# Small matrix products brought to the array's full height and width

## The chip, the cores and the metric

The kernel runs on one core of a Trainium2 chip. The time is the device time of one execution in microseconds: 2515.39 as the median of three runs (2513.62 to 2515.6). A profile was taken of one execution.

## The reference

Two transformer blocks over 256 tokens, model width 2048, float32. The first block puts 16 meta tokens ahead (272 positions). Its layer A is a differential attention: 8 heads, two score maps each of head size 128, `w = softmax(s0) - lambda * softmax(s1)`, times values of size 256, a norm, a gate, an output projection. Its layer B is an attention with sinks: 32 query heads of size 64, 4 key heads, four chunks of 64 queries; a chunk sees the 16 meta tokens and up to three chunks of keys, so 80, 144, 208 and 208 keys:

```python
sr = jnp.einsum('bnqkgd,bnskd->bnkgqs', qr, kb).astype(jnp.float32) * scale
pr = sink_softmax(sr, sink[None, None, :, :, None, None])
orr = jnp.einsum('bnkgqs,bnskd->bnqkgd', pr.astype(v.dtype), vb).reshape(B, S, D_MODEL)
```

The second block mixes a stick-breaking attention, a forgetting attention (4 heads of 128 each) and an RWKV-7 recurrence of 16 heads of size 64, whose decay and rate come from two low-rank products over 64 features (`tanh(wd) @ w_up`, `ad @ a_up`). Then come branch and output projections and an MLP of width 8192.

## The kernel before

**Main products.** The weights come as units of 2048 x 128 (one DMA of 1 MB each). ACT rounds a quarter of a unit to a short format (`wh`), DVE subtracts it (`wl`), and PE sums high x high, high x low and low x high products for every block of 128 rows (`unit_mm`, line 689). A product with both operands in the short format (F32R) is one instruction; an unsplit float32 product is two, called passes below. Main products have 128 rows, 128 columns of weights and 272 or 256 moving columns. Up to eight quarters of split weights can lie ready (WBUFS).

**Side work.** The attentions and the recurrence are generators that are moved on between main products; each `yield` is a place where another may go on. The order is made when the program is written out: each engine runs its calls in the order they are made, and `tick` (line 486) keeps an estimate of each engine's clock that decides when a step or a split of weights may follow. `limit` (line 598) finishes all but some pieces of a kind at once, whatever the clock says.

**Shapes on PE.** A form such as 64*128 in the trace means 64 rows (the summed dimension, on the partitions) and 128 columns of weights. The places that the change touches:

- `g_av` (949) and `g_attn_a` (965), layer A. The scores of the first 16 queries are a product with 16 columns of weights and 16 moving columns. The parts of the values and of the weights of the first 16 keys (high, low, high) are stacked to 48 rows, transposed as blocks of 48 columns, for the 16 queries as a block of 16 rows, and multiplied as a 48-row F32R product at the head of each half of the weighted sum.
- `e_kk` (1149), `g_bk` (1164), `g_q` (1207), `g_attn_b` (1223), layer B. For the chunks 0 and 1 the scores are unsplit 64-row products. For the chunks 2 and 3 the query's high and low parts are stacked to 128 rows and meet the key's high parts, which stand twice; then the query's high parts alone, 64 rows, meet the key's low parts. Both take 256 moving columns, more than the 208 that are used. In the weighted sum the last 16 keys of chunk 1 are a product of 16 rows; all its products have 64 columns, two heads beside each other.
- `e_lo` (1390), `g_r1` (1514). The two up projections are each a 128-row product (weights' high and low parts against the features' high parts, which stand twice) and a 64-row one (weights' high parts against the features' low parts).

In time the layers follow each other: layer A's heads run beside its own projections, layer B's beside its query and gate units (16 pairs of heads, `g_attn_b` once a pair), the recurrence's first stage beside its eight `rr`, `rk`, `rv` groups.

Of the kernel before, what the change touches and what calls it, by code (L numbers as in the profile page):

```python
# [20 lines left out]
S = 256  # L21
# [10 lines left out]
# the sets of function tables that hold a function  # L32
# [155 lines left out]
def unit_rows(inp, kind, i):  # L188
    """the unit's weights as [16 * 128 rows, 128 columns]"""
# [16 lines left out]
def const_arrays():  # L206
# [32 lines left out]
    # stage 1 of the recurrence: causal masks of the chunk products, chunk starts  # L239
# [7 lines left out]
    # stick-breaking and forgetting attention  # L247
# [8 lines left out]
def prepare(inp):  # L256
# [37 lines left out]
    # a head's rows of the forget sums' high and low parts  # L294
# [17 lines left out]
class _Eng:  # L312
    """an engine's builders, with a running estimate of when each call ends"""
# [26 lines left out]
class Prog:  # L340
# [40 lines left out]
    def rel(self, n=1):  # L381
        """the last use of n side banks is out"""
        self.live -= n
# [34 lines left out]
    def mm(self, out, lhsT, rhs, start=True, stop=True, beside=False):  # L418
        """beside: in the array's other columns, while the product before it runs"""
# [43 lines left out]
    def split_to(self, n):  # L463
        """the weights' first n pieces are split"""
        while self.done < n:
            if self.high == self.done:
                self.split_high()
            self.split_low()

    def fill(self):  # L470
        """split the weights: what is needed soon, and further while the engines are idle"""
# [12 lines left out]
    # Each engine runs its calls in the order they are made.  The estimate of every  # L484
    # engine's clock decides when a piece of side work may follow the main products.
    def tick(self, eng, attr, args, kw):
        out = kw.get("out", args[0] if args else None)
        if eng == "PE":
# [4 lines left out]
            else:  # L493
                n = _free(out)
                cost = 25.0 if self.beside else 110.0 * n / 256 if kw["rhs"].dtype == F32R else max(1.69 * n, 105.0 if _free(kw["lhsT"]) <= 64 else 213.0)
# [30 lines left out]
    def wait(self, ns):  # L526
        """the piece's next part follows a transfer of about this long"""
# [5 lines left out]
    # how many pieces of a kind may be under way together  # L533
# [33 lines left out]
    def room(self, n):  # L567
        """side work goes on until n side banks are free"""
# [3 lines left out]
    def step_gens(self):  # L572
        """move the side work on as far as its inputs are ready by now"""
# [24 lines left out]
    def limit(self, names, n):  # L598
        """let at most n pieces of such side work stay unfinished"""
# [9 lines left out]
    def run(self):  # L609
        nsub = NSUB  # L610
        self.raw, self.wsplit, self.free = {}, {}, []
        # when the first units' pieces have come
# [3 lines left out]
        # units taken together where their moving operand comes late  # L616
# [8 lines left out]
        for group in groups:  # L625
            jobs = []
            for v in group:
# [11 lines left out]
                if "join" in spec:  # L639
                    # the unit goes on with the sums of the one before  # L640
# [48 lines left out]
    def unit_mm(self, kb, b, job, w):  # L689
        """a block's products: high x high, high x low, low x high"""  # L690
# [3 lines left out]
        if spec.get("flip"):  # L694
# [5 lines left out]
            if v >= len(self.order) - 2:  # L700
                # the last units end one half of the tokens before they take up the other
# [20 lines left out]
    def evacuate(self, force=False):  # L722
        """the finished units' products leave PSUM, once their token scales are there"""
# [6 lines left out]
    def start(self):  # L730
# [25 lines left out]
        # a layer's operand comes later to this room  # L756
# [40 lines left out]
    def g_scalars(self):  # L797
        """-lambda and the scaled copies of subln's gain and of the sinks"""
# [33 lines left out]
    def newton(self, y, x):  # L832
        """one step of y -> x ** -0.5"""
# [15 lines left out]
    def tok_rsqrt(self, x):  # L849
        """x ** -0.5 for a small tile with tokens on the partitions"""  # L850
# [15 lines left out]
    def tok_spread(self, ps, dg, blocks):  # L866
        """ps[:, block] = the block's scales, on every partition"""
# [3 lines left out]
    def rsqrt_ps(self, out, ps, scale, eps_col):  # L871
        """out = (ps * scale + eps) ** -0.5"""
# [33 lines left out]
    def x_ak(self, i):  # L906
        d = self.x_A(i)
        if i == 0:
            # a quarter of the operand is there before the products, the next ones go on beside them
# [4 lines left out]
    def rope_evac(self, out, ps, t0, n, quads):  # L914
        """out = rope(ps * R) for the token columns t0..t0+n"""
# [21 lines left out]
    def e_av(self, i, ps):  # L937
# [4 lines left out]
        if f == 0:  # L942
            self.avt[h] = self.t("avt", [128, 2, 2, 128], bufs=2), self.t("av16", [48, 2, 128], F32R)
# [5 lines left out]
    def g_av(self, h, f, vT):  # L949
        # the parts of the first 16 tokens, to meet high, high and low  # L950
        v3 = self.t("av3", [128, 48], F32R)
# [5 lines left out]
        self.tr(pv[0:48, 256:384], v3.bitcast(F32), 128)  # L957
# [4 lines left out]
        self.act(self.avt[h][1][:, f, :], pv[0:48, 256:384], AF.Copy)  # L962
        self.rel()

    def g_attn_a(self, h):
# [4 lines left out]
        for j in range(2):  # L970
# [4 lines left out]
            self.mm(s[0:16, 416:432], q[:, 0:16], k[:, 0:16])  # L975
# [31 lines left out]
        w3 = self.t("aw3", [128, 3, 48], F32R)  # L1007
# [11 lines left out]
        self.tr(p2[0:48, 0:16], w3[0:16, 2], 16)  # L1019
        self.tr(p2[0:48, 16:144], w3[:, 0], 128)  # L1020
        self.tr(p2[0:48, 144:272], w3[:, 1], 128)
        yield
        wt = self.t("awt", [128, 384], bufs=1)
        w16 = self.t("aw16", [48, L], F32R, bufs=1)
        self.act(wt, p1[:, 0:384], AF.Copy)
        self.act(w16, p2[0:48, 0:L], AF.Copy)
# [44 lines left out]
    def g_gate(self, i, G, h, f):  # L1071
# [4 lines left out]
        # 2 * G * sigmoid(G)  # L1076
# [57 lines left out]
    # key columns are kept in the order chunk 0, meta, chunk 1, 2, 3: the keys of every  # L1134
    # chunk's queries are then one run of columns
# [3 lines left out]
    def rope_b(self, ps, t0):  # L1139
        """the two terms of rope(ps * R) for the tokens from t0 on"""  # L1140
# [8 lines left out]
    def e_kk(self, i, ps):  # L1149
        if i == 0:  # L1150
            self.finish(self.tabs)
            self.bk = self.t("bk", [64, 4, L], bufs=1)
            # high parts, twice in the rows, and low parts
            self.bkh = self.t("bkh", [128, 4, L], F32R, bufs=1)
            self.bkl = self.t("bkl", [64, 4, L], F32R, bufs=1)
        t, tmp = self.rope_b(ps, 0)
        self.mul(tmp, tmp, self.SR)
        for hh in range(2):
            hs = slice(64 * hh, 64 * hh + 64)
            for a, b, o in self.SEGS:  # L1160
                self.add(self.bk[:, 2 * i + hh, a:b], t[hs, o:o + b - a], tmp[hs, o:o + b - a])
        self.spawn(self.g_bk(slice(2 * i, 2 * i + 2)))

    def g_bk(self, ks):
        yield
        for j in range(2):
            self.act(self.bkh[64 * j:64 * j + 64, ks], self.bk[:, ks], AF.Copy)
        self.sub(self.bkl[:, ks], self.bk[:, ks], self.bkh[0:64, ks].bitcast(F32))
# [38 lines left out]
    def g_q(self, i, t, tmp):  # L1207
        yield
        self.mul(tmp, tmp, self.SR[:, NM:])
        q = self.t("bq", [64, 4, 2, 64], bufs=3)  # L1210
# [4 lines left out]
        # the later chunks' high and low parts, stacked  # L1215
        qs = self.t("bqs", [128, 2, 128], F32R, bufs=3)
        q2 = q[:, 2:4].rearrange("p c e x -> p c (e x)")
# [3 lines left out]
        self.bgen[i] = self.spawn(self.g_attn_b(i, q, qs))  # L1221

    def g_attn_b(self, i, q, qs):
        """two heads: rows are (head, query of the chunk)"""
# [4 lines left out]
        s = [s0[:, 0:80], s0[:, 80:224], s0[:, 224:432], s1[:, 48:256]]  # L1229
        for c, (a, b) in enumerate(self.KEYS[0:2]):  # L1230
            self.mm(s[c], q[:, c].rearrange("p e x -> p (e x)"), self.bk[:, kv, a:b])
# [972 lines left out]
```

## Time and profile before

| | |
|---|---|
| median of three runs | 2515.39 us |
| profiled execution, span | 2513.7 us |
| PE busy | 2475.5 us (98%), 19842 matmuls |
| DVE busy | 1706.6 us (68%) |
| ACT busy | 1413.9 us (56%) |
| POOL busy | 186.0 us (7%) |
| DMA | 452.66 MB, 180 GB/s |

The busy time of a matmul runs from its start to a modelled end, and matmuls overlap: a main product of 256 columns is shown with some 280 ns and followed by the next after some 118 ns. What one costs is therefore read from the starts. All instructions carry the line of one helper (L325), so they are told apart by their tiles: `pg` is the sum of a main product, `ps` of a side product.

### The profile page before, as it was taken

Reading aid. Unit: us, or ns where it says so; the run is one execution under the profiler, and the core shown is the slowest. Engines: PE = TensorE matmul, PEld = TensorE weight load, DVE = VectorE, ACT = ScalarE, POOL = GpSimd, SP = SyncE. Lnnn points to the kernel's source line nnn. Section 1 sums busy time; section 2 is a strip of 40 time slices with the busy share of each in tenths; the row PEclk is TensorE's granted clock in tenths of the full one; section 3 lists DMA queues with packets and bytes.
Section 4 is the critical chain, followed back from the end, with each engine's and each line's share of the span. In section 5 each row is a group of like instructions: output and inputs, shape, how many; then the busy total and the mean of one; then the engine's idle time right before and its main releaser. Section 6 shows DMA issues by size and latency. Waiting matters only on the chain.

```text
span 2513.7 us, 50471 instructions
## 1 busy us (share of the span) xinstructions
PE 2475.5 (98%) x19842; PEld 2358.2 (94%) x19842; DVE 1706.6 (68%) x3347; ACT 1413.9 (56%) x2888; POOL 186.0 (7%) x230
## 2 busy tenths in 40 slices
PE   8999999999999999999999999999899999999998
PEld 7999999999999999999999999999899899899886
DVE  8666676667777667777795568766765666666665
ACT  5555555557666667666555436445655455455444
POOL 5110001010000120000000100111200000000002
PEclk9999999999999999999999999999999999999999
DMA  6344444543333454667645764755455555555553
GB/s 232 138 165 151 152 153 154 181 173 135 135 135 135 168 196 174 202 203 226 216 179 174 235 195 171 279 213 186 151 185 184 186 188 192 190 185 185 188 191 125
DMA packets 123647, 452.66 MB, mean 180 GB/s; under 512 B 54704, under 2 KB 65968, under 8 KB 73872
## 3 DMA queue, kind: packets, MB, share of 16 engines
q1 hardware_dynamic: 123216, 449.24, 50.8%
q8 instruction: 156, 2.56, 0.4%
q14 instruction: 83, 0.68, 0.1%
q0 software_dynamic: 192, 0.18, 0.0%
HBM read 431.55 MB, written 17.83 MB: 179 GB/s over the span
## 4 chain that ended last, share of the span: by engine, by line
PE 96%; DVE 2%; ACT 0%; DMA 0%; issue 0%; POOL 0%; DVEq 0%; SPq 0%; ACTq 0%; POOLq 0%
PE pg L325 79%; PE ps L325 18%; DVE wl L325 0%; DMA h<-in_h_dram 0%; DVE xml L325 0%; DVE h L325 0%; DVE acc L325 0%; ACT wh L325 0%; DVE pr L325 0%; DVE xl L325 0%; ACT uj L325 0%; ACT xh L325 0%; ACT xmh L325 0%; DVE nt L325 0%; POOL gl L325 0%
## 5 line engine op out<-in xcount | busy, mean ns | idle before, releaser
L325 DVE TENSOR_TENSOR wl<-wr,wh 128x512 fp32r<-128x512 f32 x1556 | 1076.1, 709 | 549.6 <-ACT wh L325 514.8
L325 ACT ACTIVATE wh<-wr 128x512 fp32r<-128x512 f32 x1556 | 949.6, 626 | 587.9 <-PE pg L325 377.2
L325 PE MATMUL pg<-x2h,wh 128*128 128x256 f32 x1584 | 451.2, 285 | 0.0
L325 PE MATMUL pg<-x2l,wh 128*128 128x256 f32 x1584 | 445.2, 281 | 0.0
L325 PE MATMUL pg<-x2h,wl 128*128 128x256 f32 x1584 | 445.1, 281 | 0.0
L325 PEld LDWEIGHTS pg<-x2h,wh 128*128 128x128 f32 x1584 | 299.1, 189 | 3.4
L325 PEld LDWEIGHTS pg<-x2h,wl 128*128 128x128 f32 x1584 | 299.4, 189 | 0.2 <-DVE wl L325 0.2
L325 PEld LDWEIGHTS pg<-x2l,wh 128*128 128x128 f32 x1584 | 297.9, 188 | 0.0
L325 PE MATMUL pg<-xh,wh 128*128 128x272 f32 x992 | 290.6, 293 | 7.1 <-ACT xh L325 7.1
L325 PE MATMUL pg<-xh,wl 128*128 128x272 f32 x992 | 288.1, 290 | 4.5 <-DVE wl L325 4.5
L325 PE MATMUL pg<-xl,wh 128*128 128x272 f32 x992 | 287.2, 290 | 0.8 <-DVE xl L325 0.8
L325 PE MATMUL pg<-xmh,wh 128*128 128x256 f32 x1008 | 284.1, 282 | 3.1 <-ACT xmh L325 3.1
L325 PE MATMUL pg<-xml,wh 128*128 128x256 f32 x1008 | 285.0, 283 | 1.6 <-DVE xml L325 1.6
L325 PE MATMUL pg<-xmh,wl 128*128 128x256 f32 x1008 | 284.5, 282 | 1.3 <-DVE wl L325 1.3
L325 PEld LDWEIGHTS pg<-xmh,wh 128*128 128x128 f32 x1008 | 191.5, 190 | 3.8 <-ACT xmh L325 3.5
L325 PEld LDWEIGHTS pg<-xh,wh 128*128 128x128 f32 x992 | 187.6, 189 | 7.2 <-ACT xh L325 7.1
L325 PEld LDWEIGHTS pg<-xmh,wl 128*128 128x128 f32 x1008 | 191.7, 190 | 1.5 <-DVE wl L325 1.5
L325 PEld LDWEIGHTS pg<-xml,wh 128*128 128x128 f32 x1008 | 190.4, 189 | 2.7 <-DVE xml L325 2.3
L325 PEld LDWEIGHTS pg<-xh,wl 128*128 128x128 f32 x992 | 187.4, 189 | 5.2 <-DVE wl L325 5.1
L325 PEld LDWEIGHTS pg<-xl,wh 128*128 128x128 f32 x992 | 187.7, 189 | 2.2 <-DVE xl L325 2.1
L325 PE MATMUL pg<-xbh,wh 128*128 128x256 f32 x512 | 148.2, 289 | 0.0
L325 PE MATMUL pg<-yl,wh 128*128 128x272 f32 (+1 forms) x512 | 145.9, 285 | 0.3 <-DVE yl L325 0.3
(404 smaller groups left out, 4844.1 us busy)
## 6 DMA issues: line engine op xcount, KB each, us to landing
wr<-in_w_dram SPq DMA_DIRECT2D x386, 1024.0 KB, 4.8
dGt<-G SPq DMA_DIRECT2D x48, 128.0 KB, 4.8
gl<-dGt SPq DMA_DIRECT2D x16, 384.0 KB, 5.4
dW<-r1w SPq DMA_DIRECT2D x32, 128.0 KB, 4.8
x_w<-dW SPq DMA_DIRECT2D x8, 512.0 KB, 4.1
wr<-in_w_dram SPq DMA_DIRECT2D x12, 256.0 KB, 5.5
h<-in_h_dram SPq DMA_DIRECT2D x8, 272.0 KB, 5.5
w<-in_w_dram SPq DMA_DIRECT2D x4, 512.0 KB, 6.9
```

What stands on the lines that cost most here:

```text
L325: return f(*args, **kw)
```

## The change

No side product of the attentions and of the recurrence's up projections keeps 16, 48 or 64 rows:

- layer A's stacks go from 48 to 80 rows, with zeros in the last 32 (POOL writes them); the 16 queries' block is transposed as 128 rows, of which the later transposes overwrite the rest; the 16 queries' scores are made with 128 columns of weights.
- layer B's scores are split products for all four chunks, of 128 rows: the stacked query parts meet the key's high parts and then its low parts, which now also stand twice. That adds the product of low with low. The moving columns are just those used. The keys' unsplit tile holds two heads and one buffer, so `e_kk` finishes `g_bk` of the pair before.
- the 16-row product of layer B's weighted sum gets 80 rows, with zeros between the chunks' weights.
- the up projections' low parts stand twice and meet all 128 rows of the weights.
- the tile of the forget sums takes the place of one that `g_r1` uses, so `e_rv` finishes `g_f` and `g_c` before its first unit.
- the planner's price of a split product no longer falls under 256 columns.

The rest of the diff takes out comments. Its core:

```diff
-  cost = 25.0 if self.beside else 110.0 * n / 256 if kw["rhs"].dtype == F32R else ...
+  cost = 25.0 if self.beside else 110.0 * max(n / 256, 0.98) if kw["rhs"].dtype == F32R else ...
 # g_av, g_attn_a
-        v3 = self.t("av3", [128, 48], F32R)
+        v3 = self.t("av3", [128, 80], F32R)
+        self.nc.gpsimd.memset(v3.bitcast(F32)[:, 48:80], 0.0)
-        self.tr(pv[0:48, 256:384], v3.bitcast(F32), 128)
+        self.tr(pv[0:80, 256:384], v3.bitcast(F32), 128)
-            self.mm(s[0:16, 416:432], q[:, 0:16], k[:, 0:16])
+            self.mm(s[:, 416:432], q[:, 0:128], k[:, 0:16])
-        w3 = self.t("aw3", [128, 3, 48], F32R)
+        w3 = self.t("aw3", [128, 3, 80], F32R)
+        nc.gpsimd.memset(w3.bitcast(F32), 0.0)
-        self.tr(p2[0:48, 0:16], w3[0:16, 2], 16)
-        self.tr(p2[0:48, 16:144], w3[:, 0], 128)
-        self.tr(p2[0:48, 144:272], w3[:, 1], 128)
+        self.tr(p2[0:80, 0:128], w3[:, 2], 128)
+        self.tr(p2[0:80, 16:144], w3[:, 0], 128)
+        self.tr(p2[0:80, 144:272], w3[:, 1], 128)
-        w16 = self.t("aw16", [48, L], F32R, bufs=1)
+        w16 = self.t("aw16", [80, L], F32R, bufs=1)
 # e_kk, g_bk
-            self.bk = self.t("bk", [64, 4, L], bufs=1)
-            self.bkl = self.t("bkl", [64, 4, L], F32R, bufs=1)
+            self.bkl = self.t("bkl", [128, 4, L], F32R, bufs=1)
+        self.limit(("g_bk",), 0)
+        bk = self.t("bk", [64, 2, L], bufs=1)
-        self.sub(self.bkl[:, ks], self.bk[:, ks], self.bkh[0:64, ks].bitcast(F32))
+        for j in range(2):
+            self.sub(self.bkl[64 * j:64 * j + 64, ks], bk, self.bkh[0:64, ks].bitcast(F32))
 # g_q, g_attn_b
-        qs = self.t("bqs", [128, 2, 128], F32R, bufs=3)
-        q2 = q[:, 2:4].rearrange("p c e x -> p c (e x)")
+        qs = self.t("bqs", [128, 4, 128], F32R, bufs=3)
+        q2 = q.rearrange("p c e x -> p c (e x)")
-        for c, (a, b) in enumerate(self.KEYS[0:2]):
-            self.mm(s[c], q[:, c].rearrange("p e x -> p (e x)"), self.bk[:, kv, a:b])
-        for c, (o, a) in enumerate(((s0[:, 224:480], 0), (s1[:, 0:256], 16))):
-            self.mm(o, qs[:, c], self.bkh[:, kv, a:a + 256], stop=False)
-            self.mm(o, qs[0:64, c], self.bkl[:, kv, a:a + 256], start=False)
+        for c, (a, b) in enumerate(self.KEYS):
+            self.mm(s[c], qs[:, c], self.bkh[:, kv, a:b], stop=False)
+            self.mm(s[c], qs[:, c], self.bkl[:, kv, a:b], start=False)
+        p = self.t("bp", [128, 704])
+        nc.gpsimd.memset(p[:, 224:288], 0.0)
-        self.tr(blk(p2[0:16], 3), P[1][:, 128:144], 128)
+        self.tr(blk(p2[0:80], 3), p[:, 208:288], 128)
-                                   ((v[:, 0], blk(w1, 0)), (v[0:16, 2], blk(w2[0:16], 3))),
+                                   ((v[:, 0], blk(w1, 0)), (v[0:80, 2], blk(w2, 3))),
 # e_lo, g_r1
-                self.sub(self.ll[js], lo[js], self.lh[js, j].bitcast(F32))
+                for k in range(2):
+                    self.sub(self.ll[64 * k:64 * k + 64, j], lo[js], self.lh[js, j].bitcast(F32))
-            self.mm(o[:, 0:S], self.ups[js, j, sl], self.ll[js], start=False)
+            self.mm(o[:, 0:S], self.ups[:, j, sl], self.ll[:, j], start=False)
 # g_f, e_rv
-        n = self.t("nf", [128, 2, S], bufs=1)
+        n = self.t("r1p", [128, 2, S])
-            self.limit(("g_ups",), 0)
+            self.limit(("g_ups", "g_f"), 0)
+            self.limit(("g_c",), 0)
```

## Rows read from the trace of the kernel before

**Rows 1.** First lines of the page: span, busy time and share of each engine.

```profile
span 2513.7 us, 50471 instructions
PE 2475.5 (98%) x19842; PEld 2358.2 (94%) x19842; DVE 1706.6 (68%) x3347; ACT 1413.9 (56%) x2888; POOL 186.0 (7%) x230
```

**Rows 2.** Busy times in a stretch, second layer's attention: us, PE, PEld, DVE, ACT, POOL, clock.

```profile
590.00:830.00 240.00, 240.00 (x2137) 221.63 (x2137) 170.46 (x437) 155.29 (x436) 0.00 (x0) 1.00 0.38 138
```

**Rows 3.** Order of time on PE, recurrence's sums: start, us, engine, tiles, rows*columns.

```profile
981.25 0.28 PE L325 MATMUL pg<-x2h,wl 128*128 128x256 f32 x1
981.37 0.40 PE L325 MATMUL ps<-r1p,bd 128*128 128x256 f32 x2
981.60 0.38 PE L325 MATMUL ps<-ident,vmix 128*128 128x128 f32 x2
...
981.94 0.28 PE L325 MATMUL pg<-x2l,wh 128*128 128x256 f32 x1
```

**Rows 4.** Order of time on PE, a score block of the second layer.

```profile
703.10 0.28 PE L325 MATMUL pg<-xbh,wl 128*128 128x256 f32 x1
...
703.97 0.38 PE L325 MATMUL ps<-bkh,bqs 128*128 128x256 f32 x1
704.28 0.38 PE L325 MATMUL ps<-bkl,bqs 64*128 64x256 f32 x1
...
705.45 0.28 PE L325 MATMUL pg<-xbl,wh 128*128 128x256 f32 x1
```

**Rows 5.** Order of time on PE, a block of the forgetting attention.

```profile
1319.15 0.28 PE L325 MATMUL pg<-x2h,wl 128*128 128x256 f32 x1
...
1319.41 0.31 PE L325 MATMUL ps<-nc,sel 128*128 128x128 f32 x1
...
1320.73 0.28 PE L325 MATMUL pg<-x2l,wh 128*128 128x256 f32 x1
```

**Rows 6.** Order of time on PE, second layer's weighted sum, then the recurrence's chain.

```profile
700.44 1.33 PE L325 MATMUL ps<-bw,bv 80*64 80x64 f32 x28
...
701.92 0.28 PE L325 MATMUL pg<-xbl,wh 128*128 128x256 f32 x1
...
1428.04 1.15 PE L325 MATMUL ps<-x_x,x_w 128*64 128x64 f32 x32
...
1429.35 0.28 PE L325 MATMUL pg<-x2l,wh 128*128 128x256 f32 x1
```

**Rows 7.** Order of time on PE, weighted sum of the first layer.

```profile
73.76 0.29 PE L325 MATMUL pg<-xh,wl 128*128 128x272 f32 x1
73.98 0.39 PE L325 MATMUL ps<-aw,av 48*128 48x272 f32 x1
...
76.36 0.29 PE L325 MATMUL pg<-xl,wh 128*128 128x272 f32 x1
```

**Rows 8.** Order of time on PE, up projections of the recurrence.

```profile
968.75 0.28 PE L325 MATMUL ps<-lh,ups 128*128 128x256 f32 x1
...
970.12 0.28 PE L325 MATMUL pg<-x2l,wh 128*128 128x256 f32 x1
```

**Rows 9.** Order of time on PE, scores of the first layer and three transposes.

```profile
58.38 0.29 PE L325 MATMUL pg<-xh,wl 128*128 128x272 f32 x1
...
60.50 0.29 PE L325 MATMUL ps<-ident,av 128*48 128x128 f32 x1
...
60.97 0.29 PE L325 MATMUL pg<-xl,wh 128*128 128x272 f32 x1
```

**Rows 10.** Order of time on ACT, DVE and PE, keys of the second layer.

```profile
573.27 1.33 ACT L325 ACTIVATE bkh<-bk 64x544 fp32r<-64x544 f32 x2
...
575.27 0.71 DVE L325 TENSOR_TENSOR bkl<-bk,bkh 64x544 fp32r<-64x544 f32 x1
...
573.60 0.39 PE L325 MATMUL pg<-kh,wl 128*128 128x272 f32 x1 [0.89 <-DVE wl L325]
```

**Rows 11.** Longest waits: who waits for whom, us in total, times, longest.

```profile
POOL aosq L325 <- ACT aosq L325: 179.8, 8, 29.7
```

More of the change, by code (lines that the diff above doesn't have):

```diff
@@ L494, in tick @@
                 n = _free(out)
-                cost = 25.0 if self.beside else 110.0 * n / 256 if kw["rhs"].dtype == F32R else max(1.69 * n, 105.0 if _free(kw["lhsT"]) <= 64 else 213.0)
+                cost = 25.0 if self.beside else 110.0 * max(n / 256, 0.98) if kw["rhs"].dtype == F32R else max(1.69 * n, 105.0 if _free(kw["lhsT"]) <= 64 else 213.0)
         elif "act_table" in attr:
@@ L942, in e_av @@
         if f == 0:
-            self.avt[h] = self.t("avt", [128, 2, 2, 128], bufs=2), self.t("av16", [48, 2, 128], F32R)
+            self.avt[h] = self.t("avt", [128, 2, 2, 128], bufs=2), self.t("av16", [80, 2, 128], F32R)
         self.spawn(self.g_av(h, f, vT))
@@ L961, in g_av @@
         self.act(self.avt[h][0][:, :, f, :], pv[:, 0:256].rearrange("p (a b) -> p a b", a=2), AF.Copy)
-        self.act(self.avt[h][1][:, f, :], pv[0:48, 256:384], AF.Copy)
+        self.act(self.avt[h][1][:, f, :], pv[0:80, 256:384], AF.Copy)
         self.rel()
@@ L1018, in g_attn_a @@
         p2 = self.psum()
-        self.tr(p2[0:48, 0:16], w3[0:16, 2], 16)
-        self.tr(p2[0:48, 16:144], w3[:, 0], 128)
-        self.tr(p2[0:48, 144:272], w3[:, 1], 128)
+        self.tr(p2[0:80, 0:128], w3[:, 2], 128)
+        self.tr(p2[0:80, 16:144], w3[:, 0], 128)
+        self.tr(p2[0:80, 144:272], w3[:, 1], 128)
         yield
         wt = self.t("awt", [128, 384], bufs=1)
-        w16 = self.t("aw16", [48, L], F32R, bufs=1)
+        w16 = self.t("aw16", [80, L], F32R, bufs=1)
         self.act(wt, p1[:, 0:384], AF.Copy)
-        self.act(w16, p2[0:48, 0:L], AF.Copy)
+        self.act(w16, p2[0:80, 0:L], AF.Copy)
         self.rel(2)
@@ L1160, in e_kk, with g_bk @@
             for a, b, o in self.SEGS:
-                self.add(self.bk[:, 2 * i + hh, a:b], t[hs, o:o + b - a], tmp[hs, o:o + b - a])
-        self.spawn(self.g_bk(slice(2 * i, 2 * i + 2)))
-    def g_bk(self, ks):
+                self.add(bk[:, hh, a:b], t[hs, o:o + b - a], tmp[hs, o:o + b - a])
+        self.spawn(self.g_bk(slice(2 * i, 2 * i + 2), bk))
+    def g_bk(self, ks, bk):
         yield
         for j in range(2):
-            self.act(self.bkh[64 * j:64 * j + 64, ks], self.bk[:, ks], AF.Copy)
-        self.sub(self.bkl[:, ks], self.bk[:, ks], self.bkh[0:64, ks].bitcast(F32))
+            self.act(self.bkh[64 * j:64 * j + 64, ks], bk, AF.Copy)
+        for j in range(2):
+            self.sub(self.bkl[64 * j:64 * j + 64, ks], bk, self.bkh[0:64, ks].bitcast(F32))
     def e_kv(self, i, ps):
@@ L1209, in g_q @@
         self.mul(tmp, tmp, self.SR[:, NM:])
-        q = self.t("bq", [64, 4, 2, 64], bufs=3)
+        q = self.t("bq", [64, 4, 2, 64])
         for e in range(2):
@@ L1220, in g_q, with g_attn_b @@
         self.sub(qs[64:128], q2, qs[0:64].bitcast(F32))
-        self.bgen[i] = self.spawn(self.g_attn_b(i, q, qs))
-    def g_attn_b(self, i, q, qs):
+        self.bgen[i] = self.spawn(self.g_attn_b(i, qs))
+    def g_attn_b(self, i, qs):
         nc = self.nc
@@ L1228, in g_attn_b @@
         s0, s1 = self.psum(), self.psum()
-        s = [s0[:, 0:80], s0[:, 80:224], s0[:, 224:432], s1[:, 48:256]]
-        for c, (a, b) in enumerate(self.KEYS[0:2]):
-            self.mm(s[c], q[:, c].rearrange("p e x -> p (e x)"), self.bk[:, kv, a:b])
-        for c, (o, a) in enumerate(((s0[:, 224:480], 0), (s1[:, 0:256], 16))):
-            self.mm(o, qs[:, c], self.bkh[:, kv, a:a + 256], stop=False)
-            self.mm(o, qs[0:64, c], self.bkl[:, kv, a:a + 256], start=False)
+        s = [s0[:, 0:80], s0[:, 80:224], s0[:, 224:432], s1[:, 0:208]]
+        for c, (a, b) in enumerate(self.KEYS):
+            self.mm(s[c], qs[:, c], self.bkh[:, kv, a:b], stop=False)
+            self.mm(s[c], qs[:, c], self.bkl[:, kv, a:b], start=False)
         yield
@@ L1241, in g_attn_b @@
         self.act(m[:, 2], m[:, 0], AF.Exp, bias=self.prm("sinks", i))
-        p = self.t("bp", [128, 640])
-        o = 0
+        p = self.t("bp", [128, 704])
+        nc.gpsimd.memset(p[:, 224:288], 0.0)
         P = []
-        for c, (a, b) in enumerate(self.KEYS):
+        for c, (o, (a, b)) in enumerate(zip((0, 80, 288, 496), self.KEYS)):
             P.append(p[:, o:o + b - a])
-            o += b - a
             self.act(P[c], s[c], AF.Exp, scale=0.125, bias=m[:, 0, c:c + 1], accum_out=m[:, 1, c:c + 1])
@@ L1268, in g_attn_b @@
         self.act(w1, p1[:, 0:384], AF.Copy)
-        self.act(w2[:, 0:384], p2[0:80, 0:384], AF.Copy)
-        self.act(w2[0:16, 384:512], p2[0:16, 384:512], AF.Copy)
+        self.act(w2, p2[0:80], AF.Copy)
         self.rel(2)
@@ L1422, in e_lo @@
             self.lh = self.t("lh", [128, 2, S], F32R, bufs=1)
-            self.ll = self.t("ll", [128, S], F32R, bufs=1)
+            self.ll = self.t("ll", [128, 2, S], F32R, bufs=1)
             self.r1w = [self.bigt(F32, "r1w").rearrange("p a b -> p (a b)") for _ in range(2)]
@@ L1525, in g_r1 @@
         for j, o in enumerate((yp, ap_)):
-            js = slice(64 * j, 64 * j + 64)
             self.mm(o[:, 0:S], self.ups[:, j, sl], self.lh[:, j], stop=False)
-            self.mm(o[:, 0:S], self.ups[js, j, sl], self.ll[js], start=False)
+            self.mm(o[:, 0:S], self.ups[:, j, sl], self.ll[:, j], start=False)
         self.act(sq, k, AF.Square, scale=self.prm("k_k", p))
```

## The prediction

> **What bounds the kernel now.** I read the page's first part, then one stage's busy times, then the order of time on PE around the products that the change touches. The page says that PE is busy for 98% of the span [rows 1]. In the second layer's attention (590 to 830 us) PE never rests and runs at the full granted clock, while DVE is busy for 170.46 of 240 us and ACT for 155.29 [rows 2]. So in the stages touched the end time is the sum of what PE's instructions take, one after the other, and a nanosecond saved on PE there is saved at the end, as long as the splits of the weights on DVE and ACT keep up. Busy times of matmuls overlap, so I price a block of side products by starts: from the last main product before it to the second main product after it, less two main distances (0.118 us at 256 columns: three starts from 981.25 to 981.60 [rows 3]; by the same count 0.125 at 272).
>
> The view in order of time then shows what the change is about. In a block made of full 128-row products alone, two products of split parts, two transposes and the next two mains fit without a seam: 981.37 to 981.94 is 0.57 us, that is 3 x 0.118 + 2 x 0.108 [rows 3]. In the scores of the second layer, where 64-row and 128-row products alternate, products of the same size stand 0.31 us apart (703.97 to 704.28), and the next main product is late as well [rows 4]. At 0.118 for such a product, some 0.19 us is lost wherever the height changes.
>
> **The change, part by part** (all sums are PE time, per profiled execution).
>
> (1) Scores of the second layer, 16 blocks. One costs 705.45 - 703.10 - 0.236 = 2.11 us [rows 4]: two unsplit 64-row products, two passes each, and four split ones that change height each time. Afterwards there are eight split products of full height, over 80, 80, 144, 144 and four times 208 columns. The trace has no split product under 256 columns in layer B; the nearest are two at 128 columns in the forgetting attention. Its block costs 1320.73 - 1319.15 - 0.236 = 1.34 [rows 5] and holds four passes of unsplit products (two at 128 columns, two at 256), four split products (two at 128, two at 256) and two transposes. With 0.108 for a pass or transpose at 128 columns (0.00085 us a column) and twice that at 256, 0.86 goes to these, and 0.48 is left for four split products: 0.12 each, the short ones as dear as the long ones. I take 0.118 for all eight: 0.94 a block, so 1.17 x 16 = 18.7 us less. From below: if the short ones cost by their columns (1280 in all), 0.59 a block and 24.3 less. From above: if they cost two passes of an unsplit product each (0.218 at least), 2.34 a block, and 3.7 us more than now.
>
> (2) Weighted sum of the second layer, 16 blocks. Two 16-row products (four passes) stand among 80-row and 128-row ones; they become 80 rows, with zeros behind. From the first side product to the second main after: 1.48 us for 28 passes now; the recurrence's block of 32 passes, all of 128 rows, takes 1.31 [rows 6]. If 80 rows count as full height (of all the change's new heights this is the smallest, and nothing else in it holds without that), 28 such passes take 1.31 less four passes of between nothing and 1.31/32 = 0.041: 1.15 to 1.31. The saving is 0.17 to 0.33 a block; I take 0.28: 4.5 us less (2.7 to 5.3).
>
> (3) Weighted sum of the first layer, 8 blocks: 76.36 - 73.76 - 0.25 = 2.35 us, with a 48-row product at the head of each half [rows 7]. With 80 rows each half is 0.125 + 2 x 0.216 + 2 x 0.108 = 0.77, both 1.55: 0.80 less, 6.4 us in all.
>
> (4) The recurrence's up projections, 8 blocks of four products: 970.12 - 968.75 = 1.37 us to the second main after [rows 8]; five distances of 0.118 make 0.59. 0.78 less, 6.2 us in all.
>
> (5) Scores of the first layer, 8 blocks. One costs 60.97 - 58.38 - 0.25 = 2.34, with three transposes at its end (0.32) [rows 9]. Eight long passes at 0.00085 us a column take 1.42, so the two products of 16 rows and 16 columns take 0.30 each now; two passes of 128 columns of weights take 0.22. 0.08 x 16 = 1.3 less (0 to 2).
>
> (6) Transposes of 48 columns, and one of 16 rows a head. From a 48-column transpose to the second main after it are 0.47 us (60.50 to 60.97) [rows 9], of which 0.125 is a main distance and 0.216 two full transposes, so it takes 0.13 against 0.108, and widening it to 80 columns gives 0.02 each, 0.6 for all 32. The 16-row one changes height; at most twice 0.19 a head is to be had, less a pass of 0.108 in place of a shorter one. I take 1.0 us less in all (0 to 2.5).
>
> The Trainium skill ("TensorEngine Tiling (Array Packing)", Key Properties, with Available Configurations) says that a change of the tiling mode drains the engine, and counts up to 64 columns as a mode of its own. By it the 48-column transposes would drain as the 48-row products do, and the sum would be some 0.19 x 32 = 6 us larger; the row's 0.13 speaks against that for transposes, and I leave it out of the sum; its chance stands within that of the cheap products below, whose time it nearly shares.
>
> Sum of PE: 18.7 + 4.5 + 6.4 + 6.2 + 1.3 + 1.0 = 38.1 us less.
>
> (7) What it adds elsewhere. The second pair of key heads now may not be added until the first pair is copied and subtracted, since there is one buffer. On DVE stand ahead of the weights' low parts, in this order: a copy on ACT (0.66 us each) to be waited for, and two subtractions of 0.71 [rows 10]: 2.1 us. There is no cover: at this place PE already waits 0.89 us for a low part (573.60) [rows 10], so I count 2.1 whole. Behind it main products queue on PE, nothing else is late. The forget sums' pieces are forced out before the first value unit of the recurrence in the same manner, with an exchange between DVE and ACT; no row shows it, so I take the same 2.1, between 0 and twice that. The other additions (wider copies and subtractions of the queries, 16 of each, at most 0.66 and 0.71 as in rows 10; POOL's zeroing) I cost at nothing: layer B's PE time falls to 240 - 23.2 = 217 us, DVE's rises to at most 182, ACT's to at most 166, so PE covers them; were that cover gone, it would be these 11 us each. The planner's new price for short split products shifts its clock by some 0.05 us for each of the forgetting attention's eight; I take the order of emission as it was, at nothing.
>
> Net: 38.1 - 4.2 = 33.9 us off the profiled execution's 2513.7, 2479.8. The median of the three runs, 2515.39, stands 1.7 us above that span, so 2481.5.
>
> **Rivals.**
> Short split products cost as unsplit ones: the scores get 3.7 us dearer instead of 18.7 cheaper, 2481.5 + 22.4 = 2503.9. For it: none of these sizes was seen. Against: the 0.12 of [rows 5].
> Short split products cost by their columns: 5.6 us more saved, 2475.9. Against: the same row. The Trainium skill ("TensorE: Matmul & The Clock Gate", Back-to-back issue gap) gives some 81 ns for a sustained stream at 128 columns; by that eight would take 0.65 us and the end would be near 2477; the row's 0.12 decides against it.
> DVE and ACT take back half of layer B's gain (the share of DVE rises from 71% to up to 84%): 11.6 us back, 2493. For it: PE waits for low parts at 573.60 already, where both engines are fullest. Against: PE is never idle in [rows 2].
> The other side: POOL's zeroing of the first layer's weight parts holds ACT. It stands in POOL's queue behind the sum of squares, for which POOL waits up to 29.7 us at a time, 179.8 in 8 times [rows 11]; ACT's copy, and behind it the weights' high parts, would wait for it. It would have to stop PE for over (33.9 + 5.0)/8 = 4.9 us a head to end above 2520; at 6 us a head it gives 2529. Against: those waits are for pieces that are emitted later than the zeroing's inputs; POOL is free otherwise.
>
> **How the numbers follow.** The forecast 0.70, by itself 2475 to 2488; short products dear 0.08; cheap 0.07; DVE and ACT 0.12; POOL 0.03. 2473 to 2494 holds the first, the third and the fourth but for their tails, a little over 8 in 10. This kernel's runs cannot tell less than 0.2% (5 us) from no change. Faster by more than that: all but POOL and a rest, 0.95; within it 0.02; slower 0.03.
>
> **What would show it.** Right: no gap of 0.31 between split products in the scores; a score block near 0.95 us, the weighted sums near 1.2 and 1.55, the up projections 0.47; layer B some 23 us shorter. Wrong: eight score products further apart than 0.12, or new waits of PE for low parts in layer B. Step 7 shows as a wait of some 3 us where PE now waits 0.89.

## The result, and the profile after

The changed kernel takes 2493.8 us as the median of four runs (2492.66 to 2497.02); the kernel before, run beside it, 2514.51 (2513.37 to 2515.6). The ratio is 0.9918 [0.9904, 0.9932]: faster, by 20.7 us. The forecast was 2481.5, so 12.3 us of the expected gain are missing; the time lies at the upper end of the range, 2473 to 2494.

The first lines of the page after answer to [rows 1]:

```profile
span 2491.8 us, 50488 instructions
PE 2444.7 (98%) x19842; PEld 2356.4 (95%) x19842; DVE 1716.2 (69%) x3351; ACT 1417.3 (57%) x2872; POOL 193.5 (8%) x270
```

There are as many matmuls as before. PE is busy for 31 us less, but the span is only 21.9 us shorter. Where the rest went is read from the stages. Each stage begins with the first product of its own main tile, the chain's with the first score product of the stick-breaking attention; layers A and B end with the first product of their output projections. The views by tile give first and last start (here after "x count: shortest/mean/longest"), keys, layer B and recurrence:

```profile
L325 PE MATMUL pg<-kh,wh x64: 286/290/432, 542.0 to 572.3; 128*128 128x272 f32 x64
L325 PE MATMUL pg<-xbh,wh x512: 276/280/388, 572.7 to 799.1; 128*128 128x256 f32 x171
L325 PE MATMUL pg<-x2h,wh x1584: 276/280/580, 892.3 to 1556.6; 128*128 128x256 f32 x198
```

In the kernel before these three begin at 551.3, 578.4 and 921.5, the chain's stage at 1216.3 (1193.7 after). With the same view for the other tiles the stages have these lengths (us, one profiled execution each, as all lengths of stages below):

| stage | before | after | difference | forecast |
|---|---|---|---|---|
| layer A | 447.3 | 438.3 | -9.0 | -8.7 |
| keys of layer B | 27.1 | 30.7 | +3.6 | +2.1 |
| layer B's attention | 251.5 | 227.9 | -23.6 | -23.2 |
| recurrence, first stage | 294.8 | 301.4 | +6.6 | -4.1 |
| recurrence's chain, stick-breaking, forgetting | 362.4 | 363.3 | +0.9 | 0 |
| all else | | | -0.4 | 0 |

One stage stands out: the recurrence's first, 10.7 us worse than forecast. The others together are off by 1.3.

**The products.** The order of time on PE after, for one block of each kind: scores of layer A, weighted sum of layer A, scores of layer B, weighted sum of layer B, up projections (start, duration, engine, tiles, rows*columns):

```profile
58.26 0.29 PE L325 MATMUL pg<-xh,wl 128*128 128x272 f32 x1
...
60.62 0.29 PE L325 MATMUL pg<-xl,wh 128*128 128x272 f32 x1
...
73.89 0.29 PE L325 MATMUL pg<-xh,wl 128*128 128x272 f32 x1
...
75.71 0.29 PE L325 MATMUL pg<-xl,wh 128*128 128x272 f32 x1
...
590.47 0.28 PE L325 MATMUL pg<-xbh,wl 128*128 128x256 f32 x1
590.58 0.20 PE L325 MATMUL ps<-bkh,bqs 128*128 128x80 f32 x1
...
591.59 0.27 PE L325 MATMUL pg<-xbl,wh 128*128 128x256 f32 x1
...
605.23 1.03 PE L325 MATMUL ps<-bw,bv 80*64 80x64 f32 x28
...
606.42 0.28 PE L325 MATMUL pg<-xbl,wh 128*128 128x256 f32 x1
...
946.05 0.28 PE L325 MATMUL ps<-lh,ups 128*128 128x256 f32 x1
...
946.64 0.28 PE L325 MATMUL pg<-x2l,wh 128*128 128x256 f32 x1
```

Counted as in the prediction, the layer B score block is 591.59 - 590.47 - 0.236 = 0.88 us (2.11 in [rows 4]); its weighted sum 1.19 (1.48 in [rows 6]); layer A's weighted sum 75.71 - 73.89 - 0.25 = 1.57 (2.35 in [rows 7]), its scores with three transposes 2.11 (2.34 in [rows 9]); the up projections 0.59 to the second main product (1.37 in [rows 8]). In none of these blocks do split products stand 0.31 apart any more. The clock in layer B stays full, as in [rows 2]:

```profile
590.00:800.00 210.00, 210.00 (x2079) 206.91 (x2079) 165.21 (x426) 152.53 (x409) 2.12 (x14) 1.00 0.41 148
```

**The stops.** PE now stops at three places where it hardly stopped before. For the keys (where [rows 10] had 0.89 us), and twice in the recurrence's first stage (brackets: idle time before, and what ended it):

```profile
566.79 0.39 PE L325 MATMUL pg<-kh,wl 128*128 128x272 f32 x1 [3.37 <-DVE wl L325]
...
568.11 0.43 PE L325 MATMUL pg<-kh,wh 128*128 128x272 f32 x1
568.34 0.43 PE L325 MATMUL pg<-kl,wh 128*128 128x272 f32 x1
...
1014.63 0.28 PE L325 MATMUL ps<-r1p,bd 128*128 128x256 f32 x1
1017.13 0.39 PE L325 MATMUL ps<-r1p,bd 128*128 128x256 f32 x1 [2.23 <-DVE r1p L325]
1017.45 1.64 PE L325 MATMUL ps<-r1w 64*64 64x64 f32 x32
...
1159.68 0.58 PE L325 MATMUL ps<-r1p,bd 128*128 128x256 f32 x1 [4.80 <-ACT r1p L325]
1161.10 0.58 PE L325 MATMUL ps<-r1p,bd 128*128 128x256 f32 x1 [0.83 <-DVE r1p L325]
```

The first stop in the recurrence (call it the merged block) is one run of side products of the recurrence's pairs: sums over a head's rows (`ps<-r1p,bd`), chunk products (`ps<-r1w`), transposes and the next pair's up projections. They stand in one run because `e_rr` finishes the oldest pair (`limit(("g_r1",), 2)`) when nothing of it has been placed between main products. The second begins on DVE. In order of time on DVE, and on SP's queue:

```profile
1146.05 1.28 DVE L325 TENSOR_TENSOR wl<-wr,wh 128x512 fp32r<-128x512 f32 x2
1157.41 0.42 DVE L325 TENSOR_TENSOR G<-pg,R 128x256 f32<-128x256 f32 x1 [10.08 <-DMA dGt<-G]
```

```profile
1145.80 0.58 SPq L1611 DMA_DIRECT2D dW<-r1w  x1
...
1152.70 2.58 SPq L1619 DMA_DIRECT2D dBk<-bt  x4
1155.32 3.31 SPq L1978 DMA_DIRECT2D dGt<-G  x3
```

DVE stands for 10.08 us before it may write the gates' tile `G`, which has two buffers: the store that empties one (`dGt<-G`) is issued at 1155.32, behind 12 stores of the recurrence's pairs that SP issues from 1145.80 on. Behind DVE wait the low parts of the weights and the pair's squares (`r1p`), and PE with them, for 4.80 and 0.83 us.

After a stop PE may go on at half speed. Windows around the keys' stop, the merged block, and the end of the second stop with what follows it (us, busy PE, PEld, DVE, ACT, POOL, granted clock, DMA share, GB/s):

```profile
566.60:570.50 3.90, 3.71 (x18) 3.71 (x19) 3.90 (x10) 1.45 (x3) 0.00 (x0) 0.59 0.36 101
1014.40:1021.00 6.60, 4.38 (x48) 3.93 (x47) 2.98 (x6) 2.37 (x5) 0.00 (x0) 0.76 0.78 273
1157.60:1164.40 6.80, 3.89 (x38) 3.25 (x39) 6.35 (x14) 3.74 (x8) 0.00 (x0) 0.52 0.58 183
```

A clock of 0.5 is 1.2 instead of 2.4 GHz: at 568.11 the main products stand 0.23 us apart instead of 0.125.

### The profile page after: what moved, and what is told of

Its sections match the earlier page's. It is cut to its first block, busy times and chain, and to the rows that moved or that the text cites. A ratio compares the mean times of both kernels' runs of the same rounds, so it can differ in the third digit from the quotient of the medians.

```text
span 2491.8 us, 50488 instructions
## 1 busy us (share of the span) xinstructions
PE 2444.7 (98%) x19842; PEld 2356.4 (95%) x19842; DVE 1716.2 (69%) x3351; ACT 1417.3 (57%) x2872; POOL 193.5 (8%) x270
## 4 chain that ended last, share of the span: by engine, by line
PE 94%; DVE 4%; ACT 1%; issue 1%; DMA 1%; SPq 0%; DVEq 0%; POOL 0%; ACTq 0%; POOLq 0%
PE pg L325 78%; PE ps L325 16%; DVE wl L325 1%; DMA h<-in_h_dram 0%; ACT wh L325 0%; DVE pr L325 0%; DVE xml L325 0%; DVE h L325 0%; DVE acc L325 0%; DVE rtmp L325 0%; DVE xl L325 0%; DVE ti L325 0%; DVE r1p L325 0%; DVE r1w L325 0%; ACT L325 0%
## 5 line engine op out<-in xcount | busy, mean ns | idle before, releaser
L325 PE MATMUL pg<-xh,wh 128*128 128x272 f32 x992 | 291.2, 294 | 6.9 <-ACT xh L325 6.9
L325 PE MATMUL pg<-xh,wl 128*128 128x272 f32 x992 | 288.6, 291 | 3.1 <-DVE wl L325 3.1
```

The source lines that it names most:

```text
L325: return f(*args, **kw)
```

## The experiments

Theory: every product became as cheap as forecast, and what is missing are the waits in the recurrence's first stage. Rivals: the cheaper products cost something else there, or the padding itself. First the second stop: a third buffer, and then another queue.

**A third buffer for `G`** (first stage only):

```diff
-        G = self.t("G", [128, S])
+        G = self.t("G", [128, S], bufs=self.gbufs)   # 3 in this stage, 2 after it
```

> The changed kernel with three buffers instead of two for the tile of the gates (G) in the recurrence's first stage; every engine's order is the same. Theory Q (queue): the 7.5 us that PE stands still before 1159 us come from DVE waiting for a buffer of G, whose store to memory stands in SP's queue behind twelve stores of the recurrence. Then the wait of 10.08 us of DVE is gone, the block of 9.05 us falls to some 1.5, and the time is some 7 us below the changed kernel's 2493.8: 2486 to 2488. Rival D (the DMAs land late because the memory traffic is dense there, or DVE is held by something else at once): the time stays within 2 us of 2493.8.

Measured 2486.95 (2481.24 to 2489.47), ratio to before 0.9882 [0.9869, 0.9896]; the stage takes 292.1 instead of 301.4. The profiled execution is the fastest of the four (2481.24); by the medians the buffer gives 6.9 us. On DVE, at the place of the long wait:

```profile
1144.56 0.42 DVE L325 TENSOR_TENSOR G<-pg,R 128x256 f32<-128x256 f32 x1 [1.60 <-PE pg L325]
...
1152.19 0.42 DVE L325 TENSOR_TENSOR G<-pg,R 128x256 f32<-128x256 f32 x1 [0.65 <-DMA dGt<-G]
```

The 10.08 us are gone and PE does not stop there: the buffer was the limit. The merged block stays, with its wait of 2.22 us:

```profile
1016.02 0.38 PE L325 MATMUL ps<-r1p,bd 128*128 128x256 f32 x1 [2.22 <-DVE r1p L325]
1016.33 1.15 PE L325 MATMUL ps<-r1w 64*64 64x64 f32 x32
```

Here the same stop is not followed by half speed: the 32 passes take 1.15 us, against 1.64 after the like stop above. So an execution may or may not pay for it. At the keys' stop, where nothing was edited and PE waits 3.35 us, the clock stays full here too, and the keys' stage takes 29.2 instead of 30.7:

```profile
566.60:570.50 3.90, 3.76 (x29) 3.76 (x30) 3.90 (x10) 2.04 (x4) 0.00 (x0) 1.00 0.32 109
```

**Two buffers, but the store on ACT's queue:**

```diff
-        self.nc.sync.dma_start(out=self.dGt[o][:, g, :], in_=G)
+        self.nc.scalar.dma_start(out=self.dGt[o][:, g, :], in_=G)
```

> The changed kernel with the gates' stores issued from ACT's queue instead of SP's; two buffers of the gates' tile as before, the order of every engine's work the same. Theory Q (the store stood behind the recurrence's stores in SP's queue): the wait of DVE for the gates' store before 1159 us is gone although the buffers are two, the first stage of the recurrence is some 9 us shorter, 2486. Rival B (two buffers are too few for a store that takes 5 us to land in this traffic): DVE still waits several us there.

Measured 2484.53 (2483.23 to 2485.98), 0.9881 [0.9866, 0.9896]; the stage 293.6, with the merged block at half speed. With two buffers as in the changed kernel, DVE waits for no store; ACT's queue issues it between two of its copies, 0.33 us long:

```profile
1155.32 0.42 DVE L325 TENSOR_TENSOR G<-pg,R 128x256 f32<-128x256 f32 x1
```

```profile
1145.60 0.33 ACTq L325 DMA_DIRECT2D dGt<-G  x1
```

So it was not the transfer but its place in SP's queue.

**The forget sums in spare columns**, so that nothing has to be forced out before the first value unit:

```diff
-        n = self.t("r1p", [128, 2, S])
+        n = self.r1w[0][:, 2560:3072].rearrange("p (a b) -> p a b", a=2)
-            self.limit(("g_ups", "g_f"), 0)
-            self.limit(("g_c",), 0)
+            self.limit(("g_ups",), 0)
```

> The changed kernel with the forget sums in a place of their own (spare columns of the recurrence's work space), so that nothing forces them out before the first value unit; the order of emission in the recurrence's first stage moves with it. Rival F (the forced forget sums are what costs that stage its gain): both waits there go, some 11 us, 2483. Theory Q: the stores and the gates' two buffers are still there, so the stage is not reliably shorter; wherever the order lets a train of stores meet the gates' store a wait stays: 2486 to 2500, and the short wait of DVE and ACT at the first value unit goes, under 2 us.

Measured 2486.08 (2485.22 to 2486.78), 0.9881 [0.9866, 0.9896]; the stage 292.6. The second stop is gone; waits for the store of 4.4 and 5.2 us are left on DVE and stop nothing. The merged block stands, earlier:

```profile
990.19 1.04 PE L325 MATMUL ps<-r1p,bd 128*128 128x256 f32 x2 [1.94 <-ACT r1p L325]
991.16 1.97 PE L325 MATMUL ps<-r1w 64*64 64x64 f32 x32
```

So the forced forget sums brought on the second stop, by the order that follows them: in the changed kernel PE waits no more than 0.3 us at a time in this stage before the merged block, so their own exchange between DVE and ACT stops nothing. The merged block has another cause. Of the two stops one goes and one stays, which neither theory had said.

**Three pairs under way instead of two**, with a fourth buffer for the mixed inputs and the room for it taken from unused columns:

```diff
-        self.limit(("g_r1",), 2)
+        self.limit(("g_r1",), 3)
```

> The changed kernel in which a new pair of the recurrence's first stage no longer forces the third last one out (three unfinished instead of two, a fourth buffer for its inputs, its outputs in spare columns of the work space to make room). Theory L (the 3.8 us block excess near 1015 us comes from that forced end: PE's sums are put into its order before DVE has made their operand): no block there holds sums, chunk products, transposes and the next pair's projections in one, PE's wait of 2.2 us for r1p is gone, the stage is some 4 us shorter; whether the wait for the gates' buffer (7.5 us) stays depends on the order, so 2482 to 2490. Rival (that wait comes from ACT's two table loads and stays wherever the sums stand): the stage stays over 297 us or the excess only moves.

Measured 2483.69 (2481.33 to 2484.95), 0.9877 [0.9862, 0.9891]; the stage 291.2, that is 10.2 less where 4 were expected, because both stops are gone. No block is forced together: the second sums and chunk products stand between main products, at full speed, without a wait:

```profile
1015.62 0.39 PE L325 MATMUL ps<-r1p,bd 128*128 128x256 f32 x2
1015.94 1.15 PE L325 MATMUL ps<-r1w 64*64 64x64 f32 x32
```

DVE's longest wait for a store is still 7.0 us here, but PE waits no more than 0.6 us for a side product's input in the stage.

**The up projections alone**, in the kernel before (forget sums in spare columns as above, nothing forced): what moved the merged block?

```diff
-                self.sub(self.ll[js], lo[js], self.lh[js, j].bitcast(F32))
+                for k in range(2):
+                    self.sub(self.ll[64 * k:64 * k + 64, j], lo[js], self.lh[js, j].bitcast(F32))
-            self.mm(o[:, 0:S], self.ups[js, j, sl], self.ll[js], start=False)
+            self.mm(o[:, 0:S], self.ups[:, j, sl], self.ll[:, j], start=False)
```

> The kernel before with the up projections alone brought to full height (the low parts written twice, two subtractions more; the forget sums' tile laid into unused columns of the work space, so that nothing is forced out). Theory O: the planner counts the two subtractions, and that alone moves the first stage's order to the one of the kernel without the forced forget sums: the oldest pair is forced out as one block near 1015 us (layers A and B are as before, so some 25 to 30 us later than at 990), PE waits about 2 us there, the block takes 5 to 6.4 us. The stage is 6.2 shorter by its products and 3 to 4 longer by the block: 292 to 293 instead of 294.8, and the time 2512.5 (2511.5 to 2514). Rival, that the order comes from what the earlier layers' edits do to the planner's clocks: the block stands where it stood in the kernel before, without a wait, the stage takes 288.6, the time is 2508.7.

Measured 2513.18 (2511.45 to 2514.58), 0.999 [0.9982, 0.9999]; the stage 292.7, like the 292.6 of the run without forced forget sums; layers A and B are as before. PE's 2617 products of the stage stand in the same order, tile by tile, as in that run. The merged block with its wait is there, though nothing else of the change is:

```profile
1019.32 0.85 PE L325 MATMUL ps<-r1p,bd 128*128 128x256 f32 x2 [1.94 <-ACT r1p L325]
1020.09 1.59 PE L325 MATMUL ps<-r1w 64*64 64x64 f32 x32
```

**The same instructions, not counted:** the planner's clocks are set back after the added subtraction.

```diff
+                clk, dp, pv = dict(self.clk), self.dep, self.prev
                 self.sub(self.ll[64 - 64 * j:128 - 64 * j, j], lo[js], self.lh[js, j].bitcast(F32))
+                self.clk.update(clk)
+                self.dep, self.prev = dp, pv
```

> The same instructions as the run with the up projections alone, but the planner does not count the two added subtractions, so the order of the side pieces is that of the kernel before. Theory O: no wait of PE for the pair's squares before the merged block, the stage is shorter by the eight blocks' 0.78 us alone, 288.6 instead of 294.8, and the time is 2508.7 (2507.5 to 2510). Rival, that the cheaper products themselves bring the wait (PE reaches the block earlier than DVE is ready): a wait of 2 us or more of PE in the stage, 291 or more, 2511 or more.

Measured 2509.6 (2507.39 to 2510.55), 0.9975 [0.9965, 0.9985]; the stage 288.6, 6.2 less than before. PE's order in the stage is that of the kernel before, tile by tile. A merged block exists in this order too, but late, where the pair's squares are ready; first its start in the kernel before, then in this run:

```profile
1098.01 0.40 PE L325 MATMUL ps<-r1p,bd 128*128 128x256 f32 x2
```

```profile
1093.85 0.40 PE L325 MATMUL ps<-r1p,bd 128*128 128x256 f32 x2
1094.18 1.15 PE L325 MATMUL ps<-r1w 64*64 64x64 f32 x32
```

Two subtractions in the planner's account are thus worth 292.7 - 288.6 = 4.1 us (3.6 by the medians), two thirds of what the eight blocks save. Nearly all of it is the merged block, 6.26 us against 2.37, with half speed behind the stop in the former.

**Where "full height" begins:** layer A's stacks padded to 64 rows instead of 80.

```diff
-        v3 = self.t("av3", [128, 80], F32R)
+        v3 = self.t("av3", [128, 64], F32R)          # and so for its transposes, weights and products
```

> The changed kernel with the first layer's stacks padded to 64 rows (and its transposes to 64 columns) instead of 80. Theory H (PE is refilled when the height of the used part changes, and up to 64 rows count as another height than 65 to 128): the weighted sum of the first layer goes back from 1.57 to some 2.35 us a block, 8 blocks, 6 us more: 2500. Rival N (what was saved comes from the padding of the moving side, or from the order, not from a threshold between 64 and 80 rows): 2494, block 1.57.

Measured 2500.35 (2499.51 to 2502.6), 0.994 [0.9928, 0.9953]; layer A takes 444.4 instead of 438.3. One weighted sum:

```profile
73.83 0.29 PE L325 MATMUL pg<-xh,wl 128*128 128x272 f32 x1
74.05 0.39 PE L325 MATMUL ps<-aw,av 64*128 64x272 f32 x1
...
76.42 0.29 PE L325 MATMUL pg<-xl,wh 128*128 128x272 f32 x1
```

76.42 - 73.83 - 0.25 = 2.34 us, as with 48 rows. The seam is paid at 64 rows and not at 80.

**The key's low parts to full height alone**, in the kernel before:

```diff
-            self.bkl = self.t("bkl", [64, 4, L], F32R, bufs=1)
+            self.bkl = self.t("bkl", [128, 4, L], F32R, bufs=1)      # subtracted twice, once into each half
-            self.mm(o, qs[0:64, c], self.bkl[:, kv, a:a + 256], start=False)
+            self.mm(o, qs[:, c], self.bkl[:, kv, a:a + 256], start=False)
```

> The kernel before with one edit: the key's low parts stand twice and meet all 128 rows of the query's parts (this adds low with low); the unsplit products of chunks 0 and 1 stay. Theory H (the height alone): the four split products stand 0.118 us apart instead of 0.31, a score block falls from 2.11 to about 1.23 us (one drain into the 64-row products and one out of them stay), 16 x 0.88 = 14 us less: 2501. Rival U (the gain of 1.2 us a block came from replacing the unsplit products and from the fewer columns): block near 2.1, time near 2515.

Measured 2505.91 (2503.82 to 2507.11), 0.9965 [0.9952, 0.9978]: 9.0 us less, where 14 were expected. A score block:

```profile
669.75 0.28 PE L325 MATMUL pg<-xbh,wl 128*128 128x256 f32 x1
669.96 0.73 PE L325 MATMUL ps<-bk,bq 64*128 64x80 f32 x4
...
671.32 0.28 PE L325 MATMUL pg<-xbl,wh 128*128 128x256 f32 x1
```

671.32 - 669.75 - 0.236 = 1.33 us: height alone, at the same columns, takes 0.78 of the 2.11. 16 x 0.78 = 12.5, and layer B is 9.6 us shorter; two new waits at its start, 0.74 us at 580.10 and 1.40 at 585.06, are most of the rest.

**Two buffers for the unsplit keys**, so that the second pair waits for nothing:

```diff
-        self.limit(("g_bk",), 0)
-        bk = self.t("bk", [64, 2, L], bufs=1)
+        bk = self.t("bk", [64, 2 * L]).rearrange("p (h x) -> p h x", h=2)   # the query's tile shares it
```

> The changed kernel with two buffers for the unsplit keys of the second layer (the queries' tile shares them), so that the second pair is added before the first pair is split, as before the change. Theory K (the 3.5 us that PE waits for a low part of the weights among the keys' main products come from that forced order): the wait falls to about 1 us, the time by some 2.5 us to 2491. Rival (DVE is too full there in any order): within 1 us of 2493.8, the wait is still over 3 us.

Measured 2495.99 (2489.74 to 2496.72), 0.9916 [0.9902, 0.9929]: no gain, against the expectation. The keys' stage is 26.9 instead of 30.7, as expected; but layer B takes 2.2 more, which are two waits at its start (0.75 us at 571.38 for its operand, 1.41 at 576.33), and the stage of the chain 5.3 more. There `G` waits for its store again, behind the chain's loads; PE then waits 3.23 us at 1409.97 (0.80 in the changed kernel), and the granted clock is 0.86 on average from 1395 to 1420:

```profile
576.33 0.38 PE L325 MATMUL pg<-xbh,wl 128*128 128x256 f32 x1 [1.41 <-DVE wl L325]
```

```profile
1403.07 0.43 DVE L325 TENSOR_TENSOR G<-pg,R 128x256 f32<-128x256 f32 x1 [9.10 <-DMA dGt<-G]
```

**All of it:** three pairs, three buffers of `G` in the first stage and in that of the chain, two of the keys.

> The changed kernel with the three repairs together: three unfinished pairs in the recurrence's first stage, three buffers for the gates' tile there and beside the chain, two for the second layer's keys. If the gain went into these waits alone, the first stage of the recurrence takes 294.8 - 6.2 = 289 us or less, the keys' stage 27, nothing new waits elsewhere, and the time is 2480 or below. If waits move on to the next place (DVE, or SP's queue elsewhere), it stays at 2485 or above.

Measured 2479.75 (2479.29 to 2481.42), 0.9861 [0.9845, 0.9878], the fastest kernel of the study; keys 27.0, layer B 230.1, first stage 289.6, the stage of the chain 362.5. The first stage ends 0.6 above the 289 that were expected, and at the start of layer B the two waits of the run before are there again (0.73 and 1.40 us). In the first stage the clock is full and PE never rests long:

```profile
892.00:1180.00 288.00, 287.59 (x2604) 285.57 (x2604) 209.85 (x446) 198.00 (x372) 6.13 (x32) 1.00 0.65 212
```

## Why the prediction came near, and where it failed

(1) to (6), the products: right, all of them. Measured against forecast, layer B's scores take 0.89 us a block (mean of the 11 that stand alone) against 0.94, its weighted sum 1.19 against 1.20, layer A's 1.57 against 1.55; the up projections take 0.47 above two main distances, as forecast. Layer A's scores with their transposes take 0.22 less a block, 1.8 us in all against 1.3 for (5). The products of (5) are 128*16 in the trace, so they have 128 rows and what changed is their 16 columns of weights, not rows as the prediction has it. The choice in (1), short split products as dear as long ones, was right for the block: its eight of 80 to 208 columns take 0.112 each on average. That settles the first two rivals, dear and cheap products. The 64-row run shows the assumption of (2), that 80 rows count as full height.

In (6) the 48-column transposes gave nothing: a group of three transposes with one of them takes 0.341 us before and 0.338 with 80 columns (mean of 16 groups, from the first start to the second main product after it, less one main distance). So the drain at a change of the tiling mode that the Trainium skill ("TensorEngine Tiling (Array Packing)", Key Properties) states, and that the prediction carried over to these transposes, does not show on them here. The saving of (6) came from the group with the 16-row one, 0.15 a head, 1.2 us in all against 1.0.

(7), the keys: right at the full clock. PE waits 2.5 us longer than in [rows 10]; the stage is 2.1 us longer, as forecast, in the profiled executions with the third buffer and with three pairs, where the clock stays full. The profiled execution of the changed kernel has 3.6 because its clock falls behind the stop, which the term did not hold.

(7), the forget sums, and "I take the order of emission as it was, at nothing": this is the step that failed. The order did change. The planner's price, the only cause that the prediction weighed, was not what moved it: the run with the up projections alone has the old price, the run without forced forget sums the new one, and both have one order in this stage. Two subtractions, counted by the planner, moved the forced pair to a place where its squares are not ready: 4.1 us. The forced forget sums moved it again and set the recurrence's stores ahead of the gates' store on SP's queue: 301.4 - 292.6 = 8.8 us more instead of 2.1. A third buffer alone takes 9.3 off the changed kernel's stage (1.4 of them because the merged block runs at the full clock in that execution), another queue 7.8. So the stage's sum reads -6.2 + 4.1 + 8.8 = 6.7, measured 6.6; what this sum checks is that the two runs with that one order agree in time, 292.6 and 292.7.

The rivals: DVE and ACT took back next to nothing of layer B (-23.6 against -23.2), though with less work on PE they do come nearer to the bound: three runs show waits of 0.7 to 1.4 us at its start. Of POOL's zeroing there is no sign: layer A gained 9.0.

That the time lies in the range at all is luck. The forecast by itself reached up to 2488, and the range went on to 2494 for the rival "DVE and ACT" (2493), which did not come true; waits that the prediction did not hold took the time there. That nearly all of the miss was waits and the half speed behind them, and not the products, is shown by the last run. It takes 2479.75. The forecast without its own 4.2 us of waits would be 2477.3; of the 2.4 us between them, 2.1 are the two waits at the start of layer B.

The chain stage's 0.9 us is almost wholly one wait of PE, 0.80 us at 1408.95 for `zs` from ACT, which the kernel before does not have. Left open: what sets the granted clock behind a stop, and so how the missing 12 us divide between waits and half speed from one execution to the next.

## What to carry to other kernels

Where work is written out in an order that a cost estimate decides, an added instruction may move that order, however cheap it is (two subtractions, 4.1 us): compare the two orders before costing an edit at its own duration, and look at every place that finishes pending work by force. A buffer that is emptied by a store belongs to the queue that issues the store; its wait was priced here by what else stood in that queue, not by the transfer. And mixing products of up to 64 rows with 128-row ones cost more here than padding the short ones with zeros, as long as the padding needs no wait of its own.

## What the runs showed of the hardware that was not expected

- The seam between heights lies between 64 and 80 rows for these split products: 2.34 us against 1.57 for the same weighted sum.
- Eight split products of 80 to 208 columns take 0.112 us each on average, against 0.118 for one of 256. Their starts are uneven (0.04 to 0.15 apart in the block at 590.47), so the price of a single width is not shown.
- After a stop of PE of 2 to 5 us the granted clock was half for some microseconds in some executions (0.59 at the keys, 0.52 at the second stop) and full in others (the keys and the merged block with the third buffer for `G`). So such a stop has two prices: the keys' stage took 30.7 or 29.2 us, and the merged block took 6.24 us with half speed behind the stop, 4.86 with full speed (third buffer for `G`), 2.37 without the stop (subtractions not counted), each from the last main product before it to the second after, less two main distances.
- Twelve stores of 32 to 128 KB took SP from 1145.80 to 1155.32 to issue, some 0.8 us each. A load of 1 MB of weights took 0.33 there, the gates' store of 128 KB behind them 0.32 to 0.60.
